# The recurrence of a two-layer decoder trunk: a count of ScalarE's time in its instruction order, and low parts moved between engines

## The chip, the cores and the metric

The kernel runs on one core of a Trainium2 chip. The metric is the device time of one execution in microseconds (us). TensorE (PE) multiplies matrices into PSUM, VectorE (DVE), ScalarE (ACT) and GpSimd (POOL) do elementwise work, SyncE (SP) issues most DMA transfers. Each engine works off its own instructions in a fixed order and waits on semaphores for the others.

## The reference

`reference(x, ...)` is a decoder trunk of two layers over 1024 tokens of width 1024, all in float32. The first layer mixes tokens by HGRN2, a gated linear recurrence of 8 heads with 128 channels:

```python
q, f, i, g = jnp.split(h @ w_in, 4, axis=-1)
fg = lb + (1.0 - lb) * jax.nn.sigmoid(heads(f))
o = hgrn2_chunkwise(jax.nn.silu(heads(q)), 1.0 - fg, heads(i), jnp.log(fg))
o = o * lax.rsqrt(jnp.mean(jnp.square(o), -1, keepdims=True) + RMS_EPS)
o = o * g_norm_w.astype(jnp.float32) * jax.nn.silu(heads(g))
return o.reshape(B, S, D).astype(h.dtype) @ w_out
```

Here S_t = diag(f_t) S_(t-1) + k_t v_t^T and o_t = S_t^T q_t. Behind it come a residual with LayerNorm, a gated feed-forward layer (FFN) with a causal convolution, the second layer (sliding-window attention, then an FFN of the same kind), and the output.

## The kernel before, in words

**Precision.** Nearly every fp32 matrix product is made of three products of fp32r operands, `mm3` (L188): high by high (L189), high by low (L190), low by high (L191). An operand is split in two steps: ScalarE casts the high part (L171 for a weight of the recurrence, L216 elsewhere), and then another engine subtracts it from the source, which gives the low part (`low_part`, L162, instruction L164). When `low_part` is handed a list in the place of an engine, it puts the subtraction there, for VectorE, and the caller issues it later; when it is handed `nc.gpsimd`, GpSimd does it at once.

**The recurrence stage** (to about 515 us). x is loaded in 8 blocks of 128 tokens into rows of the tile Y, turned by TensorE (L199) and split into T, x transposed (`x_block`, L737). Head 0 begins with its inputs i and g (`ig_block`, L703: one projection for two token blocks, 16 mm3 of 256 columns, the first weight unit for four of the eight rows of x and the second for the other four). Then each head has two phases of four slots: `qf` (L842), four half projections of f and q of 8 mm3 of 512 columns, and four `ig_block`s. Between the mm3s stand the steps of `recur` (L871) for the same head or the one before: VectorE's products, column sums on TensorE, seven levels of `scores` with an `update` of VectorE each (L905, L907, L910) and their placement (L884), the turn of kp and its copy kd (L973), the states (L988), the head's output and its gate og (L1000). `norm` (from L1002) then takes the sums of squares on ScalarE (L1012, eight of them with a pause in the middle), the power -1/2 on GpSimd (L1014), scales og (L1016), turns it and writes it to a row of Y (L1023); for the last head it is split straight into T (L220, L221).

**What sets the order.** In these parts the order of the instructions is written by hand: the class `Order` (L56) counts a time `od.t`, which each TensorE product advances, and `od.v`, the time at which VectorE will be done. Steps that go beside the products are generators in `od.chains`; each yields how long to wait, and `od.tick()` after each mm3 resumes those that are due. `behind(us, least)` (L70) is the wait until VectorE is done, plus `us`, at least `least`. While `od.v` is within 0.5 of `od.t`, `od.fill`, that is `lay` (L1043), issues one more VectorE operation: a low part from `lowparts` whose time has come, or a subtraction on FFN weights from `pending` (L1087). ScalarE's time is not counted: the waits that go through it are constants (2.2 ahead of the products with kd, L974; 5.4 ahead of the scaling of og).

**Slots.** `slot_begin` (L1062) lays all low parts that are left, then stores and loads FFN weight units through rows of Y (one unit in a slot, two 0.5 MB loads); `slot_end` (L1091) casts the weight of a later phase on ScalarE and puts its low part into `lowparts`. Weights arrive through a ring of three raw tiles (`load`, L155, on SP) and are kept in a ring of six split tiles HL. In the last head the out weight comes through the same rings: units 0 to 2 are loaded after `qf`, unit 3 in slot 1 of the `ig_block`s; units 0 and 1 are cast in slot 0.

**The end of the stage.** `moves(tp)` (L1054) splits the normed heads 0 to 6 of two token blocks from Y into T in two steps (heads 0 to 3, then 4 to 6), with the low parts on GpSimd; the three first are begun in the last head's slots 1 to 3, the fourth ahead of the first products with the out weight. When the rows of Y are free, x is loaded into them once more for the residual (L337), and SP, behind these loads, issues those of the tiles rx (L159) and of the FFN's weights (L437). `conv_params` (L810) goes beside the heads on the ACT queue; at its end it writes a bias table of 2 MB, `rbd`, to memory (L838).

Of the kernel before, what the change touches and what calls it, by code (L numbers as in the profile page):

```python
# [22 lines left out]
NH = 8  # L23
# [31 lines left out]
class Order:  # L55
# [5 lines left out]
    def __init__(self):  # L61
        self.t = 0.0
        self.v = 0.0
        self.fill = None
        self.chains = []

    def vec(self, us, lag=0.2):
        self.v = max(self.v, self.t + lag) + us

# [38 lines left out]
def trunk(ctx: ExitStack, tc: tile.TileContext, a: dict, out: bass.AP):  # L108
# [574 lines left out]
    with tc.tile_pool(name="t", bufs=1, reuse_waits="tile") as raws, hgrn_pool as hp:  # L683
# [19 lines left out]
        def ig_block(h, us, tp, soon=None):  # L703
            if tp == 0:
                VG[h] = (hp.tile([P, NB, P], F32, name="V", bufs=2), hp.tile([P, NB, P], F32, name="G", bufs=2))
            V, G = VG[h]
            ps = psmm()
            proj_tok(us, tp, ps)
            pv = ps.rearrange("p (t g c) -> p t g c", t=2, g=2)
            ts = slice(2 * tp, 2 * tp + 2)  # L710
            nc.scalar.activation(G[:, ts, :], pv[:, :, 1, :], AF.Sigmoid)
            nc.scalar.copy(V[:, ts, :], pv[:, :, 0, :])
            def gate():
                nc.vector.tensor_tensor(G[:, ts, :], G[:, ts, :], pv[:, :, 1, :], op=ALU.mult)
                od.vec(0.4)

            if soon is None:
                gate()
            else:
                soon.append(od.later(1.2, gate))  # L720
# [10 lines left out]
        with tc.tile_pool(name="ep", bufs=1, reuse_waits="tile") as ep:  # L731
# [23 lines left out]
            with tc.manual_schedule(engines={EN.PE, EN.SP, EN.Activation, EN.DVE}):  # L755
# [6 lines left out]
                us = [ig_split(raw0)]  # L762
# [4 lines left out]
                for tb, n in ((0, 13), (1, 20)):  # L767
                    for _ in range(n):
                        nc.tensor.transpose(idle[:, :P], ident, ident)
                    x_block(tb)  # L770
                    if tb == 0:
                        us.append(ig_split(raw1))
# [16 lines left out]
                bounds = od.spawn(lower_bounds(), 4.4)  # L789
                ahead = od.spawn(x_pair(2), 2.0)  # L790
# [51 lines left out]
        def qf(h, weights):  # L842

            qs = hp.tile([P, S], F32, name="qs")
            fg = hp.tile([P, S], F32, name="fg")
            kp = hp.tile([P, S], F32, name="kp", bufs=2)
            for half in range(2):
                ts = slice(half * 512, (half + 1) * 512)
                ps = psmm()
                proj_T(weights["f"], half, ps)  # L850
                nc.scalar.activation(fg[:, ts], ps, AF.Sigmoid)
                nc.scalar.activation(fg[:, ts], fg[:, ts], AF.Identity, bias=lbt[:, 0, h:h + 1],
                                     scale=lbt[:, 1, h:h + 1])
                nc.scalar.activation(kp[:, ts], fg[:, ts], AF.Identity, bias=one[:, 0:1], scale=-1.0)
                yield
                ps = psmm()
                proj_T(weights["q"], half, ps)
                nc.scalar.activation(qs[:, ts], ps, AF.Sigmoid)

                def query(ts=ts, ps=ps):  # L860
                    nc.vector.tensor_tensor(qs[:, ts], qs[:, ts], ps, op=ALU.mult)
                    od.vec(0.7)

                if half == 0:
                    soon.append(od.later(1.2, query))
                else:
                    query()
                yield
            weights["out"] = qs, fg, kp

        def recur(h, qs, fg, kp):  # L871
# [69 lines left out]
            for i in range(2, 7):  # L941
# [3 lines left out]
                else:  # L945
# [9 lines left out]
                    def put():  # L955
                        for b in range(P // (2 * m)):
                            o = 2 * m * b
                            nc.scalar.copy(A[o:o + m, :, o + m:o + 2 * m], pv[o:o + m, :, o + m:o + 2 * m])
                update(i)
                wait = od.behind(0.6, 2.1)  # L960
                put()
                if i == 4:
                    for b in range(P // BL):
                        bs = slice(b * BL, (b + 1) * BL)
                        nc.scalar.copy(A[bs, :, bs], Ab[bs])
                yield wait
# [7 lines left out]
            yield 2.2  # L974
# [30 lines left out]
        def norm(h, pv, og):  # L1005
# [3 lines left out]
            for c in range(NB):  # L1009
                if c == NB // 2:  # L1010
                    yield 2.4
                nc.scalar.activation(junk, pv[:, c, :], AF.Square, accum_out=ss[:, c:c + 1])  # L1012
            nc.gpsimd.tensor_scalar(ss, ss, 1.0 / P, RMS_EPS, op0=ALU.mult, op1=ALU.add)
            nc.gpsimd.tensor_tensor(ss, ss, nhalf.to_broadcast([P, NB]), op=ALU.pow)  # L1014
            yield 5.4
            nc.vector.tensor_tensor(og, og, ss.unsqueeze(2).to_broadcast([P, NB, P]), op=ALU.mult)  # L1016
            od.vec(1.2)
            yield od.behind(0.5, 2.4)
# [3 lines left out]
            if h < NH - 1:  # L1022
                nc.scalar.activation(Y[:, h, :], ps, AF.Copy, scale=par[:, 80:81])  # L1023
            else:
                for t in range(0, NB, 2):
                    ts = slice(t * P, (t + 2) * P)
                    split_scaled(T[:, 0, h, ts], T[:, 1, h, ts], ps[:, ts], par[:, 80:81])
# [11 lines left out]
        def lay_low():  # L1039
            lowparts.pop(0)[1]()  # L1040
            od.vec(1.2)
# [12 lines left out]
        def moves(tp):  # L1054

            for h in (0, 4):
                while len(normed) < NH - 1 or normed[NH - 2][1] is not None:
                    yield 0.2
                Y_to_T(h, min(h + 4, NH - 1), 2 * tp, 2 * tp + 2, nc.gpsimd)
                yield 2.6  # L1060

        def slot_begin():  # L1062
            while lowparts:
                lay_low()
# [9 lines left out]
            if units and rows:  # L1074
                i, r = units.pop(0), rows[0]
# [15 lines left out]
        def slot_end(wait, *makes):  # L1091
            lows = []
            for make in makes:
                make(lows)
            for i, low in enumerate(lows):
                lowparts.append((od.t + wait + 1.0 * i, low))
# [10 lines left out]
        with tc.manual_schedule(engines={EN.PE, EN.SP, EN.Activation, EN.DVE, EN.Pool}):  # L1107
# [5 lines left out]
            for k in range(4):  # L1113
                slot_begin()
                next(steps)
                slot_end(2.0 if k % 2 else 3.4, *(make_w[k - 1:k] if k else ()))
            for _ in steps:
                pass
            ready = [(0, w["out"])]
# [11 lines left out]
            for h in range(1, NH):  # L1131
# [4 lines left out]
                for k, make in enumerate(((), make_ig[:1], make_ig[1:], ())):  # L1136
                    slot_begin()
                    next(steps)
                    slot_end(2.0 if k % 2 else 3.4, *make)
                for _ in steps:  # L1140
                    pass
                if h < NH - 1:
# [3 lines left out]
                else:  # L1146
                    oraw = [load(out_loads(rows1, 0, (2 * u, 2 * u + 1))) for u in range(3)]
                    make_w = [lambda to, u=u: out_split(oraw[u], to) for u in range(4)]
                    make_w, moved = [make_w[:2], make_w[2:3], make_w[3:], ()], []
                for tp in range(NB // 2):  # L1150
                    if tp == lead[h]:
                        ready.append((h, w["out"]))
                    slot_begin()
                    if h == NH - 1 and tp:
                        moved.append(od.spawn(moves(tp - 1), 0.8))
                        if tp == 1:
                            oraw.append(load(out_loads(rows1, 0, (6, 7))))
                    ig_block(h, us, tp, soon)
                    slot_end(2.0, *make_w[tp])
                values_in[0] = h  # L1160
                if ready:
# [4 lines left out]
            while lowparts:  # L1166
                lay_low()
            od.fill = None
            od.finish([params] + moved[:2] + soon)
            moved.append(od.spawn(moves(NB // 2 - 1), 3.0))  # L1170
            us = out_us
            begun = []
            for tb in range(4):
                begun.append(psmm())
# [3 lines left out]
            od.finish(moved)  # L1178
            ps = psax()
# [3 lines left out]
            od.finish(normed)  # L1183
# [334 lines left out]
```

## Time and profile before

| | us |
|---|---|
| median of 3 runs | 2203.21 (2203.15 to 2203.9) |
| the profiled execution | 2203.46 |
| its span in the profile | 2201.7 |
| TensorE busy in the span | 2168.1 (98%) |
| VectorE, ScalarE, GpSimd busy | 1785.0, 935.0, 126.3 |
| mean granted TensorE clock | 0.996 of full speed |

Times in a view count from the start of the span. A row of the timeline gives start, length, engine, line, operation, tile written and tiles read, and in brackets the idle time of the engine before it with what ended that. "x8" stands for eight instructions in a row. SPq and ACTq are DMA issues.

### The profile page before, as it was taken

How to read it: one execution, taken by the hardware profiler on the slowest of the kernel's cores; microseconds unless marked ns; L12 is line 12 of the kernel's file. 1: busy time of each engine (PE TensorE's matmuls, PEld its weight loads, DVE VectorE, ACT ScalarE, POOL GpSimd, SP SyncE). 2: the span in 40 equal slices, each digit the busy share in tenths (PEclk: the TensorE clock that was granted, in tenths of full speed). 3: DMA queues.
4: the chain of work that ended last, by engine and by line, in shares of the span. 5: the costliest groups of instructions: out<-in, count | busy, mean ns of one | idle time of the engine just before them, and what ended most of it. 6: DMA issues, size and time to landing. Idle time of an engine off the chain costs nothing.

```text
span 2201.7 us, 33408 instructions
## 1 busy us (share of the span) xinstructions
PE 2168.1 (98%) x13168; PEld 1811.4 (82%) x13168; DVE 1785.0 (81%) x2456; ACT 935.0 (42%) x1600; POOL 126.3 (6%) x161
## 2 busy tenths in 40 slices
PE   9999999989999999999999999999999999999998
PEld 8888888978788888887888888878888888887887
DVE  3777666565789888888998779977899888889987
ACT  3233333342744433444343456645544444343431
POOL 0000000030100000000000013211000000000001
PEclk9999999999999999999999999999999999999999
DMA  5654543244222222227854431123133222249663
GB/s 195 230 173 154 192 135 110 79 71 141 86 77 88 86 87 86 86 88 257 290 174 142 106 99 35 35 86 121 62 98 104 86 72 74 86 153 309 207 221 129
DMA packets 231972, 281.15 MB, mean 128 GB/s; under 512 B 30008, under 2 KB 160776, under 8 KB 229000
## 3 DMA queue, kind: packets, MB, share of 16 engines
q1 hardware_dynamic: 228736, 276.53, 38.8%
q10 hardware_dynamic: 2888, 2.45, 0.9%
q8 instruction: 103, 1.69, 0.3%
q14 instruction: 53, 0.43, 0.1%
q0 software_dynamic: 192, 0.04, 0.0%
HBM read 213.96 MB, written 65.01 MB: 127 GB/s over the span
## 4 chain that ended last, share of the span: by engine, by line
PE 80%; DVE 10%; ACT 3%; DMA 3%; issue 2%; POOL 1%; SPq 0%; DVEq 0%; ACTq 0%; POOLq 0%
PE psmm L189 16%; PE psmm L191 16%; PE psmm L190 16%; PE psax L191 8%; PE psax L189 8%; PE psax L190 8%; PE psax L195 3%; DVE T L164 1%; DVE HL L164 1%; PE psax L199 1%; PE psmm L195 1%; PE psax L1310 1%; DMA raw<-in_hgrn_w_out_dram 1%; ACT Y L264 1%; DMA rx<-in_ffn_w_in_dram 1%
## 5 line engine op out<-in xcount | busy, mean ns | idle before, releaser
L189 PE MATMUL psmm<-T,HL 128*128 128x512 f32 x768 | 307.2, 400 | 0.0
L190 PE MATMUL psmm<-T,HL 128*128 128x512 f32 x768 | 300.1, 391 | 2.0 <-DVE T L164 2.0
L191 PE MATMUL psmm<-T,HL 128*128 128x512 f32 x768 | 300.7, 392 | 0.0
L494 DVE SCALAR_TENSOR_TENSOR Y<-Y,cwt 128x1023 f32<-128x1023 f32 (+1 forms) x176 | 225.1, 1279 | 40.1 <-ACT Y L492 39.8
L492 ACT ACTIVATE Y<-Y,cwt 128x1024 f32<-128x1024 f32 x88 | 109.0, 1238 | 263.6 <-DVE Y L481 259.5
L189 PE MATMUL psmm<-HL,T 128*128 128x256 f32 (+1 forms) x656 | 200.1, 305 | 0.0
L191 PE MATMUL psmm<-HL,T 128*128 128x256 f32 (+1 forms) x656 | 195.7, 298 | 1.1 <-DVE T L164 1.1
L190 PE MATMUL psmm<-HL,T 128*128 128x256 f32 (+1 forms) x656 | 195.6, 298 | 0.0
L216 ACT CAST HL<-rx 128x1024 fp32r<-128x1024 f32 (+1 forms) x137 | 140.3, 1043 | 121.8 <-DMA rx<-in_ffn_w_in_dram 35.2
L164 DVE TENSOR_TENSOR HL<-rx,HL 128x1024 fp32r<-128x1024 f32 (+1 forms) x137 | 165.6, 1211 | 13.9 <-ACT HL L216 13.7
L190 PEld LDWEIGHTS psmm<-T,HL 128*128 128x128 f32 x768 | 144.4, 188 | 31.1 <-DVE T L164 2.9
L191 PEld LDWEIGHTS psmm<-T,HL 128*128 128x128 f32 x768 | 144.1, 188 | 31.1
L189 PEld LDWEIGHTS psmm<-T,HL 128*128 128x128 f32 x768 | 144.3, 188 | 30.2 <-issue 0.4
L191 PE MATMUL psax<-T,HL 128*128 128x512 f32 x352 | 137.6, 391 | 0.0
L189 PE MATMUL psax<-T,HL 128*128 128x512 f32 x352 | 137.5, 391 | 0.0
L190 PE MATMUL psax<-T,HL 128*128 128x512 f32 x352 | 137.4, 390 | 0.0
L189 PEld LDWEIGHTS psmm<-HL,T 128*128 128x128 f32 x656 | 126.9, 193 | 6.2 <-issue 2.5
L191 PEld LDWEIGHTS psmm<-HL,T 128*128 128x128 f32 x656 | 126.7, 193 | 4.7 <-DVE T L164 1.5
L190 PEld LDWEIGHTS psmm<-HL,T 128*128 128x128 f32 x656 | 127.0, 194 | 3.2
L164 DVE TENSOR_TENSOR HL<-raw,HL 128x1024 fp32r<-128x1024 f32 x52 | 63.8, 1228 | 81.0 <-ACT HL L171 80.7
L238 POOL TENSOR_TENSOR rs<-rs,nhalf 128x1 f32<-128x1 f32 x32 | 26.0, 813 | 1292.3 <-DVE rs L237 1291.8
L216 ACT CAST HT<-rx 128x1024 fp32r<-128x1024 f32 (+1 forms) x51 | 43.9, 860 | 88.5 <-PE psmm L190 30.4
(303 smaller groups left out, 5224.5 us busy)
## 6 DMA issues: line engine op xcount, KB each, us to landing
rx<-in_ffn_w_in_dram SPq DMA_DIRECT2D x136, 256.0 KB, 3.5
rx<-gd SPq DMA_DIRECT2D x118, 256.0 KB, 3.5
Y<-in_ffn_w_out_dram SPq DMA_DIRECT2D x44, 512.0 KB, 6.1
bsd<-Y SPq DMA_DIRECT2D x22, 1024.0 KB, 4.3
gd<-Y SPq DMA_DIRECT2D x44, 512.0 KB, 2.7
rx<-in_ffn_w_out_dram SPq DMA_DIRECT2D x54, 256.0 KB, 4.0
R<-bsd SPq DMA_DIRECT2D x44, 256.0 KB, 3.7
Y<-in_ffn_w_in_dram SPq DMA_DIRECT2D x40, 256.0 KB, 3.2
```

Source lines behind the costliest of these rows:

```text
L164: make = lambda e: e.tensor_tensor(lo, src, hi.bitcast(F32), op=ALU.subtract)
L189: nc.tensor.matmul(ps, st(0), mv(0), start=start, stop=False)
L190: nc.tensor.matmul(ps, st(0), mv(1), start=False, stop=False)
L191: nc.tensor.matmul(ps, st(1), mv(0), start=False, stop=stop)
L195: nc.tensor.matmul(ps, lhsT, rhs, start=start, stop=stop, **kw)
L199: nc.tensor.transpose(ps, src, ident)
L216: nc.scalar.copy(hi, src)
L238: nc.gpsimd.tensor_tensor(rs, rs, nhalf, op=ALU.pow)
L264: nc.scalar.activation(hf[:, kc, :], ps[:, k * P:(k + 1) * P], AF.Identity, bias=shift, scale=scale)
L492: nc.scalar.activation(c, u, AF.Identity, bias=cwt[:, l, 3, ci:ci + 1], scale=cwt[:, l, 2, ci:ci + 1])
L494: nc.vector.scalar_tensor_tensor(c[:, sh:], u[:, :S - sh], cwt[:, l, 2 - sh, ci:ci + 1], c[:, sh:], op0=ALU.mult, op1=ALU.add)
L1310: nc.tensor.matmul(pv[:, e, jj, lo:], q[bp // 2][es, e, qs], Kl[es, pp, ks] if low else Kh[:, pp, e, ks], start=not low and jj == 0, stop= ...
```

## The change

`Order` gets a third time, `od.a`, for ScalarE, with `od.act(us)` beside each of its operations, and three waits are worked out from it. A low part carries the time at which its cast is done by this count and a tag of the phase in which it is due (-1 for at the end of the present one). `slot_begin` lays only those that were ready 3 us ago; `lay_lows` at the end of each phase lays what is due. Up to two FFN weight units are loaded in a slot for rows first used in slots 0 and 1. The moves' low parts (eight subtractions of 256 columns by four or three heads) go to VectorE through the same list instead of to GpSimd; the last two moves begin later. Out weight unit 0 is loaded ahead of the last head's `qf` and cast in its last slot. At the start the first low part is GpSimd's, TensorE makes 40 idle transposes instead of 20 behind block 0 of x, and blocks 1 to 3 of x are turned between the first products.

```diff
@@ -61,11 +61,15 @@
         self.v = 0.0
+        self.a = 0.0
         self.fill = None
...
         self.v = max(self.v, self.t + lag) + us
+
+    def act(self, us, lag=0.2):
+        self.a = max(self.a, self.t + lag) + us
     def behind(self, us, least):
@@ -710,6 +714,7 @@
             nc.scalar.copy(V[:, ts, :], pv[:, :, 0, :])
+            od.act(0.7)
             def gate():
@@ -759,17 +764,25 @@
                     x_load(tb)
-                us = [ig_split(raw0)]
+                us = [ig_split(raw0, nc.gpsimd)]
                 lm = ep.tile([P, NH], F32, name="lm")
...
                 idle = psmm()
-                for tb, n in ((0, 13), (1, 20)):
+                for n in (13, 40):
                     for _ in range(n):
                         nc.tensor.transpose(idle[:, :P], ident, ident)
-                    x_block(tb)
-                    if tb == 0:
-                        us.append(ig_split(raw1))
+                    if n == 13:
+                        x_block(0)
+                us.append(ig_split(raw1))
+
+                def x_first():
+                    yield 0.0
+                    x_block(1)
+                    yield 2.2
+                    x_block(2)
+                    yield 0.5
+                    x_block(3)
                 def lower_bounds():
@@ -786,8 +799,8 @@
                     nc.vector.tensor_scalar(lbt[:, 1, :], lbt[:, 0, :], -1.0, 1.0, op0=ALU.mult, op1=ALU.add)
-                bounds = od.spawn(lower_bounds(), 4.4)
-                ahead = od.spawn(x_pair(2), 2.0)
+                bounds = od.spawn(lower_bounds(), 4.9)
+                ahead = od.spawn(x_first(), 0.6)
                 ig_block(0, us, 0)
@@ -852,10 +865,12 @@
                 nc.scalar.activation(kp[:, ts], fg[:, ts], AF.Identity, bias=one[:, 0:1], scale=-1.0)
+                od.act(2.1)
                 yield
...
                 nc.scalar.activation(qs[:, ts], ps, AF.Sigmoid)
+                od.act(0.6)
                 def query(ts=ts, ps=ps):
@@ -956,6 +971,7 @@
                             nc.scalar.copy(A[o:o + m, :, o + m:o + 2 * m], pv[o:o + m, :, o + m:o + 2 * m])
+                        od.act(0.7)
                 update(i)
@@ -963,6 +979,7 @@
                         nc.scalar.copy(A[bs, :, bs], Ab[bs])
+                    od.act(1.6)
                 yield wait
@@ -971,7 +988,8 @@
             nc.scalar.copy(kd, ps)
-            yield 2.2
+            od.act(1.0)
+            yield max(od.a - od.t + 0.4, 2.0)
             while values_in[0] < h:
@@ -1009,18 +1027,20 @@
                     yield 2.4
+                od.act(0.33)
                 nc.scalar.activation(junk, pv[:, c, :], AF.Square, accum_out=ss[:, c:c + 1])
...
             nc.gpsimd.tensor_tensor(ss, ss, nhalf.to_broadcast([P, NB]), op=ALU.pow)
-            yield 5.4
+            yield od.a - od.t + 3.2
             nc.vector.tensor_tensor(og, og, ss.unsqueeze(2).to_broadcast([P, NB, P]), op=ALU.mult)
             od.vec(1.2)
-            yield od.behind(0.5, 2.4)
+            yield od.behind(0.9, 2.4)
             ps = psax()
...
                 nc.scalar.activation(Y[:, h, :], ps, AF.Copy, scale=par[:, 80:81])
+                od.act(1.1)
             else:
@@ -1036,8 +1056,8 @@
         pending, soon, lowparts = [], [], []
-        def lay_low():
-            lowparts.pop(0)[1]()
+        def lay_low(i=0):
+            lowparts.pop(i)[2]()
             od.vec(1.2)
@@ -1056,12 +1076,19 @@
                     yield 0.2
-                Y_to_T(h, min(h + 4, NH - 1), 2 * tp, 2 * tp + 2, nc.gpsimd)
+                lows = []
+                Y_to_T(h, min(h + 4, NH - 1), 2 * tp, 2 * tp + 2, lows)
+                od.act(1.0)
+                lowparts.append((od.a + 0.3, tp, lows[0]))
                 yield 2.6
+        def lay_lows(first=0, ready=1e9):
+
+            for low in [low for low in lowparts if low[0] <= ready and low[1] <= first]:
+                lay_low(lowparts.index(low))
+
         def slot_begin():
-            while lowparts:
-                lay_low()
+            lay_lows(-1, od.t - 3.0)
             od.finish(soon)
@@ -1071,8 +1098,10 @@
             rows = [r for r in free if free[r] <= n <= begins[r] + 1]
-            if units and rows:
-                i, r = units.pop(0), rows[0]
+            for r in rows[:2 if n < 2 else 1]:
+                if not units:
+                    break
+                i = units.pop(0)
                 for k in range(2):
@@ -1088,12 +1117,12 @@
                 pending.append(lambda i=i, r=r, last=last: (last(), summed.append((i, r, slot_no[0]))))
-        def slot_end(wait, *makes):
-            lows = []
+        def slot_end(makes=(), due=-1):
             for make in makes:
+                lows = []
                 make(lows)
-            for i, low in enumerate(lows):
-                lowparts.append((od.t + wait + 1.0 * i, low))
+                od.act(1.05)
+                lowparts.append((od.a + 0.3, due, lows[0]))
         values_in, values_done, normed = [0], [-1], []
@@ -1113,9 +1142,10 @@
                 next(steps)
-                slot_end(2.0 if k % 2 else 3.4, *(make_w[k - 1:k] if k else ()))
+                slot_end(make_w[k - 1:k] if k else ())
             for _ in steps:
                 pass
+            lay_lows(-1)
             ready = [(0, w["out"])]
@@ -1133,54 +1163,65 @@
                 steps = qf(h, w)
-                for k, make in enumerate(((), make_ig[:1], make_ig[1:], ())):
+                make_last = []
+                if h == NH - 1:
+                    oraw = [load(out_loads(rows1, 0, (0, 1)))]
+                    make_w = [lambda to, u=u: out_split(oraw[u], to) for u in range(4)]
+                    make_last = make_w[:1]
+                for k, make in enumerate(((), make_ig[:1], make_ig[1:], make_last)):
                     slot_begin()
                     next(steps)
-                    slot_end(2.0 if k % 2 else 3.4, *make)
+                    slot_end(make, 0 if make is make_last else -1)
                 for _ in steps:
                     pass
+                lay_lows(-1)
                 if h < NH - 1:
...
                 else:
-                    oraw = [load(out_loads(rows1, 0, (2 * u, 2 * u + 1))) for u in range(3)]
-                    make_w = [lambda to, u=u: out_split(oraw[u], to) for u in range(4)]
-                    make_w, moved = [make_w[:2], make_w[2:3], make_w[3:], ()], []
+                    oraw.extend(load(out_loads(rows1, 0, (2 * u, 2 * u + 1))) for u in range(1, 3))
+                    make_w, moved = [make_w[1:2], make_w[2:3], make_w[3:], ()], []
                 for tp in range(NB // 2):
...
                     slot_begin()
+                    if h == NH - 1 and tp == 1:
+                        lay_lows()
+                        oraw.append(load(out_loads(rows1, 0, (6, 7))))
                     if h == NH - 1 and tp:
-                        moved.append(od.spawn(moves(tp - 1), 0.8))
-                        if tp == 1:
-                            oraw.append(load(out_loads(rows1, 0, (6, 7))))
+                        moved.append(od.spawn(moves(tp - 1), 0.8 if tp < 3 else 6.0))
                     ig_block(h, us, tp, soon)
-                    slot_end(2.0, *make_w[tp])
+                    slot_end(make_w[tp], -1 if h < NH - 1 else 0)
                 values_in[0] = h
+                lay_lows(-1)
                 if ready:
...
                 raise ValueError("a unit is left")
-            while lowparts:
-                lay_low()
-            od.fill = None
-            od.finish([params] + moved[:2] + soon)
-            moved.append(od.spawn(moves(NB // 2 - 1), 3.0))
+            od.finish([params] + moved[:1] + soon)
+            lay_lows()
             us = out_us
...
             for tb in range(4):
+                if tb == 2:
+                    od.finish(moved[1:2])
+                    lay_lows(1)
                 begun.append(psmm())
...
             od.finish(moved)
+            lay_lows(2)
+            moved = [od.spawn(moves(NB // 2 - 1))]
             ps = psax()
...
                 out_part(begun[tb], us, tb, range(KC - 1))
-            od.finish(normed)
+            od.finish(moved + normed)
+            lay_lows(3)
+            od.fill = None
     def ffn(l, begun, us, rows, resid, gcol, bcol, end_rows, ln):
```

## Prediction

> **What bounds the kernel now.** I read the page first (who is busy), then the busy time by stretches (where TensorE is not), then TensorE's waits and the timelines of the gaps.
>
> ```profile
> span 2201.7 us, 33408 instructions
> PE 2168.1 (98%) x13168; PEld 1811.4 (82%) x13168; DVE 1785.0 (81%) x2456; ACT 935.0 (42%) x1600; POOL 126.3 (6%) x161
> q8 instruction: 103, 1.69, 0.3%
> ```
>
> TensorE is idle for 33.6 of 2201.7 us in all. The instruction order built for both kernels differs only up to about 600 us; TensorE gets 20 more instructions, all idle transposes. So a gain can only come out of TensorE's gaps and its clock before 600 us:
>
> ```profile
> 0.00:12.00 12.00, 7.82 (x52) 7.18 (x53) 3.49 (x3) 4.73 (x6) 5.11 (x16) 0.98 0.84 275
> 12.00:25.00 13.00, 13.00 (x103) 13.00 (x102) 5.37 (x12) 5.45 (x9) 0.00 (x0) 0.89 0.89 289
> 125.00:150.00 25.00, 23.67 (x364) 17.99 (x357) 18.87 (x36) 10.58 (x17) 0.00 (x0) 1.00 0.45 155
> 150.00:425.00 275.00, 275.00 (x3078) 245.65 (x3076) 179.79 (x313) 93.04 (x218) 10.52 (x10) 1.00 0.41 138
> 450.00:475.00 25.00, 21.14 (x307) 19.18 (x306) 22.71 (x30) 9.25 (x14) 9.99 (x4) 1.00 0.60 82
> 475.00:500.00 25.00, 21.84 (x218) 19.14 (x218) 10.62 (x20) 8.99 (x15) 8.51 (x4) 0.86 0.46 127
> ```
>
> Columns: length, busy us of PE, PEld, DVE, ACT, POOL, then the granted clock. The gaps sit at the start, in head 1 (125 to 150: 1.33 us idle) and in the last head (450 to 500: 7.02 us idle, clock 0.86). Heads 2 to 6 (150 to 425) have none: nothing can be gained there, only lost.
>
> **Start.**
>
> ```profile
> 10.50 1.13 PE L199 MATMUL psax<-ident,Y 128*128 128x128 f32 x8 [2.55 <-DMA Y<-in_x_dram]
> 5.60 2.35 PE L769 MATMUL psmm<-ident 128*128 128x128 f32 x20
> 460.41 2.47 POOL L164 TENSOR_TENSOR T<-Y,T 128x1024 fp32r<-128x1024 f32 x1 [10.85 <-PE psmm L191]
> 7.26 1.05 ACT L171 CAST HL<-raw 128x1024 fp32r<-128x1024 f32 x1 [5.04 <-DMA raw<-in_hgrn_w_in_dram]
> ```
>
> Before: 2.55 us of waiting for x block 1, its 8 turns, and products from 11.35. The clock of 0.89 over the 13 us behind that wait costs 13 x 0.11 = 1.4 us, that of 0.98 over the 12 ahead another 0.2. After: 40 idle transposes last 40 x 2.35/20 = 4.7 us, to about 10.3, and close the idle time. The first product that uses a low part waits for GpSimd: cast done at 8.31, plus 2.47 (the one GpSimd split of 1024 columns shown), so about 10.9. Block 1's turns (0.85 from start to next start) move behind it, so in work done PE is 0.4 us later, plus an estimated 0.2 for block 1's low part. Sum: -1.6 + 0.4 + 0.2 = **-1.0**; bounds +0.6 (clock falls all the same) and -1.6.
>
> The Trainium skill (TensorE: Matmul & The Clock Gate, What's actually happening) has the clock fall to half after an idle window of about 3.4 us. This idle time is 2.55 us, so by the page the low clock would not be its doing, the term would be +0.6 instead of -1.0, and the time 2202.6; the row, in which the low clock follows right behind it, decides.
>
> **Head 1.**
>
> ```profile
> 125.52 1.22 DVE L1016 TENSOR_TENSOR og<-og,ss 128x1024 f32<-128x1024 f32 x1
> 126.88 1.06 PE L199 MATMUL psax<-ident,og 128*128 128x128 f32 x8 [0.59 <-DVE og L1016]
> 146.67 1.23 DVE L164 TENSOR_TENSOR HL<-raw,HL 128x1024 fp32r<-128x1024 f32 x1 [3.04 <-ACT HL L171]
> 149.24 0.95 PE L199 MATMUL psax<-ident,kp 128*128 128x128 f32 x7 [0.73 <-DVE tot L910]
> ```
>
> Two waits, 0.59 + 0.73. Products normally start 0.2 to 0.3 us ahead of the modelled end of the one before (10.50 + 1.13 against 11.35), so each costs about that more: 1.8 us together. After, the turn of og waits 0.9 instead of 0.5 behind VectorE, with one product group more ahead of it, and the low part of 1.23 us is laid after the chain's updates instead of ahead of them. Both waits go. **-1.8**; bounds 0 and -1.8.
>
> **Heads 2 to 6.** Low parts are now laid when their cast was due 3 us ago or at the end of a phase, and not at each slot's begin. Once per head the second input weight's low part now stands right behind og:
>
> ```profile
> 213.82 1.22 DVE L1000 TENSOR_TENSOR og<-psax,G 128x1024 f32<-128x1024 f32 x1 [2.24 <-PE psax L195]
> 214.33 0.27 PE L189 MATMUL psmm<-HL,T 128*128 128x256 f32 x1
> ```
>
> The first products by this weight come about 3.6 us after the start of og (0.5 us to the block, then 24 products of 0.12 us); og and the low part take 2.75. Margin 0.85: **0**. The cover is these 0.85 us; one VectorE operation of 1.2 more ahead would cost 0.35 per head.
>
> **Last head, a new wait.**
>
> ```profile
> 446.00 0.27 ACT L1012 ACTIVATE sq<-psax 128x128 f32<-128x128 f32 x1
> 447.46 0.59 ACT L858 ACTIVATE qs<-psmm 128x512 f32<-128x512 f32 x1
> 446.13 1.23 DVE L164 TENSOR_TENSOR HL<-raw,HL 128x1024 fp32r<-128x1024 f32 x1 [4.73 <-ACT HL L171]
> 446.14 0.28 PE L189 MATMUL psmm<-HL,T 128*128 128x256 f32 x1
> ```
>
> Out weight 0 is now split in this phase, so the second input weight is cast behind qs. With the four sums from 446.00 gone ahead, qs starts 1.4 earlier, at 446.0, the cast ends at 447.4 and the low part at 448.6 to 448.7 (behind og's scaling and qs on VectorE). PE begins the block at 446.14 and needs it 12 products later, at 447.6. **+1.1**; bounds 0 and +2.3 (one more VectorE operation ahead).
>
> **Last head, GpSimd, and the big transfer.**
>
> ```profile
> PE psax L195 <- issue: 4.8, 1, 4.8
> PE psax L195 <- DVE kp L907: 1.3, 1, 1.3
> PE psax L195 <- DVE tot L910: 0.6, 1, 0.6
> PE psax L195 <- DVE Ab L884: 0.4, 1, 0.4
> 463.20 7.51 POOL L164 TENSOR_TENSOR T<-Y,T 128x768 fp32r<-128x768 f32 x3 [0.32 <-ACT T L216]
> 464.22 2.00 DVE L905 TENSOR_TENSOR qp<-qp,tot 128x512 f32<-128x512 f32 x1
> 471.12 0.67 DVE L905 TENSOR_TENSOR qp<-qp,tot 128x512 f32<-128x512 f32 x1
> 456.51 0.66 ACTq L838 DMA_DIRECT2D rbd<-rl  x1
> 458.07 19.93 DMA raw<-in_hgrn_w_out_dram
> rbd<-rl ACTq DMA_DIRECT2D x1, 2048.0 KB, 25.1
> ```
>
> Beside GpSimd's subtraction the same VectorE operation takes 2.00 instead of 0.67. The eight subtractions go to VectorE: 8 x 1.2 (1024 columns) or less, about 8.5 us, and the stretching of about 7 us goes. VectorE is as full as before, but its operations come in time: the three waits (1.3 + 0.6 + 0.4) go.
>
> The largest wait, 4.8 us, waited for nothing that the profile shows. I take it for an instruction block that came late: 1.69 MB in 103 packets is 16 KB each, and 2 x 13168 TensorE instructions over 103 is one block per 256. The 2 MB transfer of rbd, issued at 456.5 and landing in 25.1 us, covers it, and the weight load issued at 458.07 took 19.93 in the same stretch. The low clock behind it (0.86 over 25 us) costs about 2 more. After, rbd is issued at the same place within 1 us (its product is untouched, one scaling less is ahead, one cast more), and the block boundary still falls some 7 us behind it. If the block comes as late after rbd as before, PE runs dry at the same instruction and goes on at the same time: the waits ahead of that point (0.4 + 1.3) are only exchanged for more dry time. What is left is the 0.6 behind it and some 0.4 by which rbd goes earlier: **-1.0**; bounds +1 (rbd later) and -9.
>
> **Behind the recurrence.**
>
> ```profile
> 492.32 5.29 SPq L337 DMA_DIRECT2D Y<-in_x_dram  x7
> 503.01 19.98 SPq L159 DMA_DIRECT2D rx<-in_hgrn_w_out_dram  x8
> 509.77 1.23 DVE L1016 TENSOR_TENSOR og<-og,ss 128x1024 f32<-128x1024 f32 x1 [5.30 <-POOL ss L1014]
> 519.87 2.95 ACT L216 CAST TX<-rx 128x1024 fp32r<-128x1024 f32 x3
> Y<-in_x_dram SPq DMA_DIRECT2D x16, 512.0 KB, 7.4
> 556.92 1.09 PE L199 MATMUL psmm<-ident,Y 128*128 128x128 f32 x8 [0.27 <-ACT Y L264]
> ```
>
> The last moved rows' low part of four heads now stands behind L1016 on VectorE: 511.0 + 1.2 = 512.2. Loads of x into those rows of Y, issued from 492 before, wait for it; SP issues in order, so the eight rx loads (from 503 before) stand behind them, at about 514, and land with them at about 520 to 522. Their casts began at 519.87: 0.6 to 2.6 us late. PE has products ready until then; the row at 556.92 shows it waiting for the next norm by 0.27, so part of the delay is seen. **+0.5**; bounds 0 and +4.
>
> **Loads moved.** Two units of the FFN's weight in one slot (heads 0 and 1) and the first out weight a phase sooner are the same transfers, earlier in SP's queue; the 16 engines' share is 0.41 to 0.45 there, and weights are loaded a phase ahead: **0**. It would cost a late cast, up to 1 us, where two 0.5 MB loads stand ahead of a 0.25 MB one.
>
> **Sum.** -1.0 - 1.8 + 0 + 1.1 - 1.0 + 0.5 = -2.2. The profiled run took 2203.46 us (span 2201.7 and 1.8 around it), 0.25 above the median of 2203.21: 2201.26 for such a run, **2201.0** as a median. Own range 2198.5 to 2204. About 0.2% (4.4 us) is what a measurement of this kernel can tell from no change.
>
> **Rivals.**
> A, *the dry time goes*: the late block was a meeting of one block with rbd's first part, and the new order misses it. For it: 102 other blocks show no such wait. Against: the boundary stays near. It gives 4.8 + 2 more: 2201.0 - 6.8 = **2194**. The Trainium skill (Runtime: NRT & Kernel Launch, Instruction fetch mechanics) says that an engine fetches its next block by itself and that the cost of a boundary is mostly hidden; by that rule this case holds, and the row of 4.8 speaks against it.
> B, *late low parts in heads 2 to 6* (slower): the low part comes two operations of 1.22 late, at each of five heads, in a stretch with no idle time to give: 5 x (2.44 - 0.85) = 8.0, so **2209**. It decides from a lateness of 0.85. For it: all low parts are laid later, VectorE is full with subtractions of 0.7 that fill its gaps. Against: the order shows og and that low part next to each other.
> C, *the queue at the end*: rx lands 2.6 late or more and the norms pass it all on: +4 in place of +0.5, **2204.5**.
> D, *nothing moves*: the estimate of ScalarE's time changes waits that were never last: start and head 1 stay, **2203**.
>
> **Chances.** Forecast 0.42, A 0.24, B 0.20, C 0.10, D 0.04. Below 2198.8: nearly all of A and a seventh of the forecast, 0.30. Above 2207.6: most of B, some of C, 0.24. Between: 0.46. The range of 2193 to 2209 leaves out some of A and of B, under 0.2.
>
> **What would show it.** Start: clock near 1.00 from 12 to 25, PE idle under 1.5 us ahead of its first product. Head 1: 25.00 busy from 125 to 150. Heads 2 to 6: 275.00 of 275. Last head: a wait of about 1 us for HL L164 near 447; none for kp, tot, Ab; one issue wait of 6 to 9 us that ends near 477. If that wait is gone, A holds; if TensorE waits for HL L164 in heads 2 to 6, B. End: rx issued near 513, and no wait over 1 us from 515 to 600.

## The result and the profile after

The changed kernel is slower: 2207.99 us median (2206.74 to 2212.86, 14 runs) against 2202.93 (2200.64 to 2206.63, 14 runs) for the kernel before; the ratio is 1.0028 (95% interval 1.002 to 1.0036). The profiled execution took 2207.85 us with a span of 2205.5, 3.8 longer than before.

The busy time by stretches of the changed kernel, with the columns as in the prediction (PEld is TensorE loading weights; the last two figures are the busy share of the DMA engines and the GB/s that they moved):

```profile
0.00:12.00 12.00, 10.44 (x73) 10.04 (x74) 2.60 (x2) 4.50 (x5) 7.50 (x17) 1.00 0.88 280
12.00:25.00 13.00, 12.66 (x110) 12.45 (x108) 5.61 (x13) 6.20 (x9) 0.00 (x0) 1.00 0.88 284
125.00:150.00 25.00, 25.00 (x355) 19.91 (x354) 17.84 (x34) 12.30 (x19) 0.00 (x0) 1.00 0.37 110
150.00:425.00 275.00, 272.95 (x3057) 243.90 (x3056) 176.66 (x311) 89.02 (x214) 9.55 (x10) 0.99 0.40 134
425.00:450.00 25.00, 24.06 (x140) 20.86 (x138) 9.17 (x17) 12.14 (x28) 1.83 (x2) 1.00 0.24 86
450.00:475.00 25.00, 22.39 (x307) 20.68 (x308) 18.85 (x32) 8.31 (x13) 0.00 (x0) 1.00 0.66 98
475.00:500.00 25.00, 21.61 (x228) 18.92 (x228) 12.18 (x22) 7.42 (x13) 0.00 (x0) 0.86 0.20 31
```

The clock at the start is full now (1.00 for 0.89), head 1 has no gap, and the stretch from 150 to 425, which had none, has lost 2.05 us and a little clock.

The two traces make the same products of split operands (three to each mm3) in nearly the same order. So they can be laid side by side by count: the time at which the n-th such product starts, after minus before.

| product | at (before), us | after minus before | made in between |
|---|---|---|---|
| 100th | 28.4 | -0.8 | start: -0.8 |
| 700th | 156.3 | -2.5 | head 1: -1.7 |
| 900th | 192.5 | +1.3 | head 2: **+3.8** |
| 1900th | 396.9 | +1.35 | heads 3 to 6: 0 |
| 2400th | 513.8 | +1.4 | last head: +0.1 |
| 2900th | 639.4 | +2.65 | behind the recurrence: +1.2 |
| 3000th | 663.1 | +3.95 | a wait near 657: +1.3 |
| last | span | +3.8 | |

TensorE's waits in the changed kernel (in total, times, longest):

```profile
PE psmm L195 <- issue: 5.9, 1, 5.9
PE psmm L195 <- DVE HL L168: 4.3, 3, 2.0
PE psmm L194 <- DVE HL L168: 1.0, 1, 1.0
PE psmm L203 <- ACT Y L268: 1.6, 2, 1.3
```

The longest for a low part (L168, L164 before) is the one in head 2. Its timelines on ScalarE, VectorE and TensorE:

```profile
166.20 1.06 ACT L175 CAST HL<-raw 128x1024 fp32r<-128x1024 f32 x1
166.69 0.68 DVE L1116 TENSOR_TENSOR Y<-Y 128x512 f32<-128x512 f32 x1
179.80 0.69 DVE L920 TENSOR_TENSOR qp<-qp,tot 128x512 f32<-128x512 f32 x1 [1.49 <-PE psax L199]
181.55 2.35 DVE L168 TENSOR_TENSOR HL<-raw,HL 128x1024 fp32r<-128x1024 f32 x2
182.82 0.50 PE L195 MATMUL psmm<-T,HL 128*128 128x512 f32 x1 [2.04 <-DVE HL L168]
184.49 0.63 PE L194 MATMUL psmm<-T,HL 128*128 128x512 f32 x1
184.91 0.63 PE L195 MATMUL psmm<-T,HL 128*128 128x512 f32 x1
```

The cast is done at 167.26, but its low part starts at 181.55: it stands at the end of the phase, together with the next one, and behind an update that itself waits for TensorE's scores. TensorE waits 2.04 us, and then its products start 0.42 apart (184.49, 184.91) instead of 0.23 (122.20 and 122.43 before): the clock has fallen, to 0.57 of full speed over the 4 us from 183, which is worth 1.7 us. Wait and clock are the 3.8.

The last head in the changed kernel, ScalarE, VectorE and TensorE, then the rbd write and the late block:

```profile
445.54 1.03 ACT L175 CAST HL<-raw 128x1024 fp32r<-128x1024 f32 x1
448.18 0.69 DVE L876 TENSOR_TENSOR qs<-qs,psmm 128x512 f32<-128x512 f32 x1 [1.38 <-ACT qs L872]
448.78 1.22 DVE L168 TENSOR_TENSOR HL<-raw,HL 128x1024 fp32r<-128x1024 f32 x1
450.06 0.38 PE L194 MATMUL psmm<-HL,T 128*128 128x256 f32 x1 [1.00 <-DVE HL L168]
456.49 0.66 ACTq L851 DMA_DIRECT2D rbd<-rl  x1
478.39 0.37 PE L195 MATMUL psmm<-HL,T 128*128 128x256 f32 x1 [5.94 <-issue]
```

No wait for kp, tot or Ab is left, and yet TensorE goes on at 478.39, 21.9 us behind the issue of rbd; before it was 477.61, 21.1 behind it. That this wait is one for instructions can be read from the trace's packets of the instruction queue (q8 on the page, 16 KB each): one starts at 454.44, the next only at 476.03, and TensorE goes on 2.36 us behind that start. In the kernel before they start at 454.58 and 475.36, and it goes on 2.25 behind the second.

And the end, SP and ScalarE:

```profile
513.59 1.75 SPq L341 DMA_DIRECT2D Y<-in_x_dram  x4
522.46 1.28 SPq L341 DMA_DIRECT2D Y<-in_x_dram  x3
530.81 1.05 ACT L220 CAST TX<-rx 128x1024 fp32r<-128x1024 f32 x1 [4.24 <-DMA rx<-in_hgrn_w_out_dram]
559.47 1.09 PE L203 MATMUL psmm<-ident,Y 128*128 128x128 f32 x8 [1.26 <-ACT Y L268]
```

The loads of x go out in two lots, the second between those of rx; the fourth cast of rx starts at 530.81 (525.63 before), and the next norm's turn waits 1.26 instead of 0.27.

### The profile page after: what moved, and what is told of

Same layout as the page of the kernel before. It is cut to its first block, busy times and chain, and to the rows that moved or that the text cites. A ratio compares the mean times of both kernels' runs of the same rounds, so it can differ in the third digit from the quotient of the medians.

```text
span 2205.5 us, 33442 instructions
## 1 busy us (share of the span) xinstructions
PE 2171.3 (98%) x13188; PEld 1814.7 (82%) x13188; DVE 1784.6 (81%) x2463; ACT 934.3 (42%) x1600; POOL 109.4 (5%) x154
## 4 chain that ended last, share of the span: by engine, by line
PE 82%; DVE 9%; ACT 3%; DMA 2%; issue 2%; POOL 1%; SPq 0%; DVEq 0%; ACTq 0%; POOLq 0%
PE psmm L193 17%; PE psmm L195 17%; PE psmm L194 17%; PE psax L195 8%; PE psax L193 8%; PE psax L194 8%; PE psax L199 4%; PE psax L203 1%; DVE T L168 1%; PE psmm L199 1%; DVE HL L168 1%; PE psax L1351 1%; DMA rx<-in_ffn_w_in_dram 1%; DVE Y L498 1%; ACT Y L268 1%
## 5 line engine op out<-in xcount | busy, mean ns | idle before, releaser
L168 DVE TENSOR_TENSOR HL<-rx,HL 128x1024 fp32r<-128x1024 f32 (+1 forms) x137 | 165.4, 1210 | 14.6 <-ACT HL L220 14.3
L194 PEld LDWEIGHTS psax<-T,HL 128*128 128x128 f32 x352 | 66.1, 188 | 14.3
```

Of the source, the lines that this page charges most:

```text
L168: make = lambda e: e.tensor_tensor(lo, src, hi.bitcast(F32), op=ALU.subtract)
L194: nc.tensor.matmul(ps, st(0), mv(1), start=False, stop=False)
```

## The experiments

**1. Head 2 alone.** One low part of the changed kernel is laid at a slot's begin, the last but one of head 2's second phase (`slot_no` still has 17 there), and even ahead of the time at which its cast is done by the count.

```diff
-            lay_lows(-1, od.t - 3.0)
+            lay_lows(-1, od.t - (-9.0 if slot_no[0] == 17 else 3.0))
```

> The changed kernel, but in the last slot but one of head 2's second phase the low part that is ready by the count is laid at the slot's begin; nothing else is edited. Theory H (the loss is made in head 2: the low part of the next weight waits for the phase's end, TensorE waits 2.04 us for it near 181, and the clock falls behind that): the wait and the half rate behind it go, the stretch from 150 to 425 is busy throughout at clock 1.00, and the time falls by 3.5 to 4, to about 2204.2. Rival G (the loss is made behind 500 us by the moves' low parts on VectorE): the wait goes, but the time falls by under 1.

2204.97 us, ratio 1.0017 (1.0008 to 1.0026). The wait is gone: 274.86 us busy from 150 to 425 at clock 1.00, and up to the 2900th product the trace gains 4.0 on the changed kernel's: 0.6 at the start, which this edit doesn't touch, 3.5 in head 2. The low part's row now starts where ScalarE is done:

```profile
166.70 1.23 DVE L168 TENSOR_TENSOR HL<-raw,HL 128x1024 fp32r<-128x1024 f32 x1 [5.12 <-ACT HL L175]
```

The median gains about 2.4 on the ratio of 1.0028, less than 3.5 to 4; with the intervals of both it can't be told whether the rest is given back. Theory H stands for the 3.8 of the trace. By the times it is not the whole loss: with head 2 mended the kernel is still slower than the kernel before, clear of the noise.

**2. Why it came late: a near miss.** The order's own count (not the trace's time) has this low part ready at 146.5 and the slot begin at 149.5, 2.95 us later, where the rule asks for 3.0; VectorE was counted full to 153.1, so the filling (`lay`) didn't take it either. The second condition matters as much as the first: in heads 3 to 5 the same low part misses the 3.0 too (2.82, 2.95 and 2.95), but VectorE is counted only 2.1 us ahead there instead of 3.7, and the filling takes it some 2 us into the slot. In the trace it then starts 5.9 us behind the end of its cast, against 14.3 in head 2, and no product waits.

```diff
-            lay_lows(-1, od.t - 3.0)
+            lay_lows(-1, od.t - 2.5)
```

> The changed kernel with one number: a slot begins by laying the low parts that were ready 2.5 us ago by the count, in place of 3.0. In head 2 the order's own count has the low part ready at 146.5 and the slot begin at 149.5, so it misses the 3.0 by less than 0.1 and waits for the end of the phase; with 2.5 it is laid at that slot's begin. If this near miss is the cause: TensorE's wait of 2.04 near 181 and the half rate behind it go, and the time falls by 3.5 to 4 from the changed kernel's (ratio to the kernel before 1.0011 to 1.0015). Rival (the low part is late whatever the rule, because VectorE is full there): the wait stays, or moves to an update of the recurrence, and the time stays within 1.

2204.58 us, ratio 1.0014 (1.0005 to 1.0023): the ratio is in the range expected (1.0011 to 1.0015), 3.1 us below the changed kernel's, and again above 1. Heads 2 to 6 are whole again:

```profile
150.00:425.00 275.00, 275.00 (x3077) 246.08 (x3075) 177.11 (x311) 92.15 (x218) 9.17 (x10) 1.00 0.40 137
```

The rival falls: VectorE had room for it.

**3. The rule of the kernel before.** All low parts at each slot's begin, ScalarE still counted.

```diff
-            lay_lows(-1, od.t - 3.0)
+            lay_lows(-1)
```

> The changed kernel, but each slot begins by laying all low parts left from the slot before, as the kernel before did; ScalarE's time is still counted. Theory H: head 2's wait goes (-3.8); head 1's two waits do not come back if the counted waits removed them (0), or come back in part if the later low parts removed them (+0.9): 2204 to 2205. Rival G: within 1 of the changed kernel.

2206.74 us, ratio 1.0024 (1.0014 to 1.0034). Head 2's wait is gone, og's wait of head 1 doesn't come back, the one for tot does:

```profile
148.78 1.06 PE L203 MATMUL psax<-ident,kp 128*128 128x128 f32 x8 [0.73 <-DVE tot L925]
```

So of head 1's two waits the counted wait removed the one for og, and the later low parts the one for tot: from the 500th to the 700th product this run gains 0.6 on the kernel before, the changed kernel 1.7. The median is 2 higher than expected; in the trace the run lies 3.1 behind the kernel before at the 3000th product, most of it made behind 560 us, and why there stays open.

**4. The moves' low parts on GpSimd again.**

```diff
-                lows = []
-                Y_to_T(h, min(h + 4, NH - 1), 2 * tp, 2 * tp + 2, lows)
+                Y_to_T(h, min(h + 4, NH - 1), 2 * tp, 2 * tp + 2, nc.gpsimd)
```

> The changed kernel, but the moves' eight low parts are GpSimd's again; the order of the moves stays as changed. Theory H: head 2 is untouched; the time moves by -1 to +1: VectorE's operations beside GpSimd are stretched again in the last head, but that is ahead of the late instruction block and is swallowed by it; the loads of x go out a few us sooner. Rival G: the low parts on VectorE behind the scaling of the last head's og hold the loads of x and rx, and cost 2.5 behind 500 us; the time falls by 2 to 3 and the waits near 557 and 657 shrink to what they were (0.4 and 0.5).

2209.12 us, ratio 1.003 (1.0019 to 1.0041). Rival G falls: the wait grows (561.71, 2.40 for 1.26), and the loads of x go out no sooner (514.70 and 524.54), where Theory H, too, had expected them a few us sooner.

```profile
561.71 0.55 PE L203 MATMUL psmm<-ident,Y 128*128 128x128 f32 x3 [2.40 <-ACT Y L268]
514.70 1.75 SPq L341 DMA_DIRECT2D Y<-in_x_dram  x4
524.54 1.28 SPq L341 DMA_DIRECT2D Y<-in_x_dram  x3
```

**5. The moves begun as before**, low parts on VectorE.

```diff
-                        moved.append(od.spawn(moves(tp - 1), 0.8 if tp < 3 else 6.0))
+                        moved.append(od.spawn(moves(tp - 1), 0.8))
...
             lay_lows()
+            last = od.spawn(moves(NB // 2 - 1), 3.0)
             us = out_us
...
-            moved = [od.spawn(moves(NB // 2 - 1))]
+            moved = [last]
```

> The changed kernel, but its last two moves begin when they did in the kernel before (0.8 us into the slot, and ahead of the first products with the out weight), so that all seven loads of x go out ahead of the loads of rx. Their low parts stay on VectorE. Theory Q (behind 500 us it is the late start of these moves that costs: the last three loads of x were issued at 522.5, between those of rx, and the fourth rx cast came 5 us late): the rx loads go out near 508 to 512, the wait near 557 falls from 1.4 to about 0.4, and the time falls by 1 to 2.5. Rival (the low parts themselves, being on VectorE, cost there): the wait near 557 stays over 1 and the time stays within 0.5.

2207.07 us, ratio 1.003 (1.0018 to 1.0042); the changed kernel on the same chip had 2209.15 and 1.0034 (1.0022 to 1.0047). All seven loads of x go out at 506.73, and the wait near 557 is gone:

```profile
506.73 3.23 SPq L341 DMA_DIRECT2D Y<-in_x_dram  x7
557.59 1.08 PE L203 MATMUL psmm<-ident,Y 128*128 128x128 f32 x8
```

From the 2400th to the 2900th product the trace gains 0.5 on the kernel before, where the changed kernel loses 1.2 and 1.9 (two profiles). The five other variants that begin these moves late lose 1.4 to 2.6 there, and the two of run 7 that begin them as before gain 0.4 and 0.6. So the cost sits in when the moves begin, and not in the engine of their low parts. By the times alone 2 us is within the intervals.

**6. The 2 MB write sooner, in the changed kernel and in the one before.** The edit starts the whole chain of `conv_params` sooner: some small loads, turns and copies, and the write at its end.

```diff
         def conv_params():
-            yield 330.0
+            yield 303.0
```

> The changed kernel, but the chain that ends in the 2 MB write of rbd begins 27 us sooner, so that the write falls into the last head's half projections, where TensorE uses up an instruction block in some 29 us, and not beside the scores. If the late block is held by that write: the wait without a releaser (5.9 us near 472 to 478) and the half rate behind it (about 2) go, and with them nothing else comes: the time falls by 7 to 8, to about 2200.5. If the late block has nothing to do with rbd (rival: TensorE's instruction supply falls short in the short products of the scores by itself): the wait stays within 1 us of 5.9.

2200.4 us, ratio 0.9996 (0.9987 to 1.0005): 7 less than the changed kernel's ratio gives. No wait without a releaser is left in the last head, and the clock is full:

```profile
450.00:475.00 25.00, 24.72 (x389) 23.48 (x390) 20.19 (x35) 9.26 (x14) 0.00 (x0) 1.00 0.25 83
475.00:500.00 25.00, 25.00 (x200) 21.61 (x200) 13.22 (x22) 9.04 (x27) 0.00 (x0) 1.00 0.01 1
```

The write is issued at 424.01 now, and it still holds instructions back: packets of q8 start at 418.27 and only then at 442.17, where the changed kernel has them at 418.93 and 432.47. But there, in the half projections, TensorE has no wait.

> The kernel before, with only the chain that ends in the 2 MB write of rbd begun 27 us sooner. If the write holds the instruction block there too: the wait without a releaser (4.75 us near 473 to 478) and the half rate behind it go, while VectorE's waits beside GpSimd (1.3, 0.6, 0.4) stay and are no longer swallowed: the time falls by 5.5 to 7, to 2195 to 2197. Rival (the wait is made by the short products of the scores alone): nothing changes.

2198.42 us, ratio 0.9983 (0.9974 to 0.9992); the span is 6.8 shorter than that of the kernel before, the median 3.5, less than the 5.5 to 7 expected. The wait of 4.75 is gone, so the rival falls. VectorE's waits beside GpSimd are no longer swallowed and even grow, to 3.9 us from 2.3, which takes part of the gain:

```profile
PE psax L195 <- DVE kp L907: 2.0, 1, 2.0
PE psax L195 <- DVE tot L910: 1.9, 1, 1.9
PE psax L195 <- issue: 1.7, 1, 1.7
```

The wait without a releaser that is left is another, 1.65 us ahead of 89.17 us, where the other profiles have none; what made it there stays open.

**7. The edits together, and the last head's low part.** First those of 1, 5 and 6.

> The changed kernel with three edits at once: head 2's low part a slot sooner, rbd 27 us sooner, the last moves begun as before. If the three costs add (3.8 + 7.3 + 1 to 2.5) the ratio to the kernel before, 1.0028 for the changed kernel, falls by 0.0055 to 0.0062, to 0.9966 to 0.9973, or by some 6 to 7.5 us against the kernel before. If a part is given back later (loads that land late let the earlier work wait, as near 1127 us), it is 0.998 to 0.9995.

2194.44 us, ratio 0.9967 (0.9954 to 0.9979): 7.5 faster than the kernel before, and the sum of the three. The kernel before gains 3.5 of that by the edit to the write alone (run 6), so some 4 us are left to the change with the other two edits, though the two intervals just overlap. The fourth edit, with 2.5 for the special case:

```diff
                 else:
+                    if h == NH - 1:
+                        lay_lows(-1)
                     query()
```

> The three edits together, with 2.5 in the place of the special case for head 2, and a fourth: in the last head the second input weight's low part is laid ahead of the product with qs, not behind it. In the changed kernel its cast ended at 446.57, VectorE then waited 1.38 for ScalarE's qs, and the low part began at 448.78; TensorE waited 1.00 for it. If the place behind qs is the cause (and not the cast): that wait goes and the time falls by 1 against the three edits, to a ratio of 0.9962 (about 0.9955 to 0.997 with the uncertainty of the times). Rival (the cast is late): the wait stays at 1.0 and the ratio at 0.9967.

2193.58 us, ratio 0.9967 (0.9956 to 0.9978). The wait is gone (25.00 busy from 425 to 450), since the low part stands ahead of qs now:

```profile
442.91 1.22 DVE L168 TENSOR_TENSOR HL<-raw,HL 128x1024 fp32r<-128x1024 f32 x1
444.77 0.69 DVE L876 TENSOR_TENSOR qs<-qs,psmm 128x512 f32<-128x512 f32 x1 [0.64 <-ACT qs L872]
425.00:450.00 25.00, 25.00 (x159) 22.46 (x158) 12.82 (x19) 10.24 (x26) 1.83 (x2) 1.00 0.86 154
```

So the place behind qs was the cause. The time is that of the three edits: 1.6 us ahead at the 2400th product, level with them at the end.

**8. The changed kernel once more.**

> The changed kernel once more, unedited, for a second profile of it and for times on the same chip as the three others. Theory: the wait of 2.04 near 181, the one of 1.0 near 449, the one of 5.9 near 472 and the wait of 1.4 near 557 stand where they were, to 0.1; those near 657 and 1134, which end on a load from memory, move by up to 1 or 2 us from one execution to the next and are no part of the change. Rival: they stand where they were as well (1.8 and 0.4), and the change makes them.

2209.15 us. The waits in head 2 (2.04), in the last head (1.0) and near 557 (1.3) stand where they were. The one without a releaser is 7.07 instead of 5.94, which the expectation had to 0.1; TensorE goes on at 480.18. The start is 0.1 ahead of the kernel before instead of 0.8. Near 657 it waits 0.75 instead of 1.63, near 1134 0.6 more than in the first profile. So most of the table's line for 657 moves from run to run; ten profiles of the changed kernel and its variants have 0.54 to 1.68 there, the two with the order of before 0.37 and 0.25, so that some tenths of it may be the change's. That stays open.

## Why the prediction was wrong

- **Heads 2 to 6: 0** is the step that failed: it is +3.8, all in head 2. The prediction looked at the one low part behind og and its margin of 0.85, which held in every head. It did not follow the low part of the next head's weight, which the new rule leaves lying when it misses "ready 3 us ago" and VectorE is counted full, until the phase ends. Runs 1 and 2 show it. Rival B had place and sign, but not the mechanism: once, for a whole wait and the clock behind it, and not five times for a part.
- **Start: -1.0**, measured -0.8 in this pair of profiles; over ten profiles of kernels with the new start from 0.0 to -1.5, mean -0.84. All of these are against one profile of the old start. In the other one, the second of run 6, x block 1 came sooner (first two rows below): TensorE waited 1.00 instead of 2.55, the clock stayed full, and the 100th product came 2.36 sooner, ahead of all ten. So a gain at the start isn't shown. That the idle time made the clock fall fits both: full behind 1.00, 0.89 behind 2.55. The Trainium skill's window of about 3.4 us (TensorE: Matmul & The Clock Gate, What's actually happening) is longer than the 2.55 us here, and than the 2.04 in head 2, behind which it fell too (0.57 from 183 to 187, third row). But that is not the same in each execution: in run 6's first kernel the same wait of 2.04 left the clock full (last two rows), and head 2 lost 2.3 instead of 3.8.

```profile
9.64 1.09 PE L199 MATMUL psax<-ident,Y 128*128 128x128 f32 x8 [1.00 <-DMA Y<-in_x_dram]
12.00:25.00 13.00, 13.00 (x114) 13.00 (x113) 6.65 (x14) 6.30 (x9) 0.00 (x0) 1.00 0.85 270
183.00:187.00 4.00, 4.00 (x28) 2.72 (x32) 1.23 (x2) 0.00 (x0) 0.00 (x0) 0.57 0.45 131
183.68 0.50 PE L195 MATMUL psmm<-T,HL 128*128 128x512 f32 x1 [2.04 <-DVE HL L168]
184.00:188.00 4.00, 4.00 (x79) 3.11 (x78) 2.12 (x4) 0.00 (x0) 0.00 (x0) 1.00 0.45 131
```

- **Head 1: -1.8**, measured -1.7, by the two causes named (run 3).
- **Last head, the new wait: +1.1**, measured +1.0 in the waits. Size and place were right; the cause named first, a cast behind qs, was wrong: the cast ended at 446.57, and it is the low part's place behind the product with qs (run 7). Nor did qs start 1.4 sooner, at 446.0: it started at 447.54, behind a wait of 0.97 us for TensorE.
- **The big transfer: -1.0.** That the waits ahead of the late block are only exchanged for more dry time is what the trace has: 5.94 for 4.75, with the other three gone, and +0.1 for the last head in all, the new wait included, so about -0.9 for this term. Its size is partly luck: over eight profiles TensorE goes on 20.2 to 23.0 us behind the issue of rbd. That rbd's write holds the block is shown by the packets of instructions and by moving the write with its chain, in two kernels (run 6). Rival A fell. The Trainium skill has the cost of a block boundary as mostly hidden (Runtime: NRT & Kernel Launch, Instruction fetch mechanics); the one beside the 2 MB write was not: it cost 4.75 to 7.1 us of waiting.
- **Behind the recurrence: +0.5**, measured +1.2, and up to +2.5 with the wait near 657. The mechanism (loads of x held, rx behind them) was right. The late point was put down to the low part's place on VectorE; runs 4 and 5 show that the later begin of the moves decides.

With head 2 at 0 the sum in the table would have been +0.2, and -1.1 without the wait near 657, in place of -2.2: the end cost more than was given to it. The times say more: with head 2 whole the kernel is still 3.1 and 3.7 us above the kernel before (runs 2 and 1). So head 2 is 2.4 to 3.1 of some 6 us by the times; the later moves are 1 to 2 us of the rest in the traces, and where what remains sits is not shown. The start, which differs between the two profiles of the old one by more than 2 us, is one place where a single profile can mislead.

## What to carry to other kernels

When a rule by which deferred work is placed is changed, list every deferred item in every repetition with its new place and the first one that needs it; one item that misses its threshold while its engine is counted full is enough (the three that missed it with room left cost nothing), and the stretch that has no idle time is where it costs most. A stall behind which another stands gives nothing when it is removed; find the last of the chain, here a large write beside the instruction stream, and move that first. A wait of 2 us on TensorE is paid nearly twice when the clock falls behind it, which it did in four of the five profiles with head 2's wait.

## What the runs showed of the hardware

TensorE ran dry for 4.75 to 7.1 us in the last head while 2 MB were written in 25 us, and a 256 KB load issued 1.6 us behind that write took 19.93 us to land. Over the eight profiles that have the write at this place, a packet of instructions started 20.8 to 22.9 us behind the one before it, with the write in between; TensorE ran dry when it had begun 536 to 546 more instructions from the start of the earlier packet, about two blocks of 256, and went on 2.2 to 2.4 us behind the start of the later one. Issued some 30 us sooner, the write held back a packet as well (19.9 to 23.9 us between two starts in four profiles, 13.5 and 14.7 at that place without it), but beside the half projections, whose products start 0.23 us apart (29 us for the 128 of a block, by this figure), that cost nothing that could be seen.

A wait of 2.04 us halved the clock for 3.4 us in four profiles of five.

A subtraction near 1125 us waited 0.84 us for its load in the kernel before and 2.21 in run 6's first kernel. There TensorE waited 2.05 us behind it and the clock fell (0.57 over 4 us): 3.8 us of the 8.4 that this profile had gained on the kernel before in the last head were lost. Its time, 2204.19, is 3.8 above the median of that run; this is one way in which single profiles and medians come to differ by some us.

```profile
1125.13 0.69 DVE L592 TENSOR_TENSOR rx<-rx,R 128x512 f32<-128x512 f32 x1 [2.21 <-DMA rx<-gd]
```
